# The first layer's mixing steps in another order, and a first softmax unit that needs only its own head's keys

## The chip, the cores and the metric

The kernel runs on one core of a Trainium2 chip. A core has a matrix engine (TensorE, in the profile PE, its weight loads PEld), a vector engine (VectorE, DVE), a scalar engine (ScalarE, ACT), a general engine (GpSimd, POOL) and a queue engine for transfers (SyncE, SP). ACT and POOL can issue transfers as well, from their own instruction queues. The metric is the device time of one execution in microseconds; the median of several runs is compared.

## The reference, cut to what matters

Two layers work on 512 latent tokens and 256 context tokens of width 1024, in float32. Each layer modulates both token sets, mixes them in three ways side by side, and then runs an MLP of width 4096.

```python
def trunk_layer(x, cx, c, c_ctx, rows, cols, w_mod, b_mod, g_mix, w_in, ..., update_ctx):
    sh1, sc1, ga1, sh2, sc2, ga2 = modulation(c, w_mod, b_mod)
    sh1c, sc1c, ga1c, sh2c, sc2c, ga2c = modulation(c_ctx[None], w_mod, b_mod)
    u = (rmsnorm(x, g_mix) * (1 + sc1) + sh1) @ w_in
    uc = (rmsnorm(cx, g_mix) * (1 + sc1c) + sh1c) @ w_in
    p, gq, gk, gv, gg, rf, rb, aq, ak, av = split_in(u)
    ...
    o_gc, s_f, s_b = gla_bidir(*gla_features(gqc, gkc, gvc, rfc, rbc, w_gate, b_gate), s_zero, s_zero)
    o_gl, _, _ = gla_bidir(*gla_features(gq, gk, gv, rf, rb, w_gate, b_gate), s_f, s_b)
    ...
    mix = jnp.concatenate([pool_mixer(p, w_pool, s_pool),
                           gla_output(o_gl, gg, g_gla, x.dtype),
                           latent_attention(ql, k_all, v_all)], axis=-1) @ w_out
    x = x + ga1 * mix
    x = x + ga2 * squared_relu_mlp(rmsnorm(x, g_mlp) * (1 + sc2) + sh2, w_up, w_down)
    ...
```

The modulation is `silu(c) @ w_mod + b_mod`, six vectors of 1024. The gated linear attention (GLA) has four heads of 64 and a data-dependent decay in both directions; the softmax attention has eight query heads and two key heads, with norms and rotary positions. The context is updated in the first layer only.

## The kernel before, in words

Float32 products are made from a high part and a low part of each operand: three matmuls per tile, of hi and hi, hi and lo, lo and hi. Weights come by SP into a `raw` buffer (three of them, 128 x 1024), ACT rounds them into a `hi` buffer, DVE subtracts into a `lo` buffer (five of each); this is `wload`, and its lines are L159 (ACT) and L78 (DVE). Most other tiles of 128 x 768 are work slots of one pool of 29; the activations hT of a mixing stage occupy 16 of them until the last projection has read them.

The mixing stage of a layer is written as four Python generators, and the string `STEPS[l]` says, letter by letter, which of them makes its next step:

- `a`, the projections: the gates of the GLA (one step each for two halves), keys and values of the softmax attention (k_proj, six token tiles, norm and rotation), its queries (q_proj, twice: Q0 and Q1), and the pooled part (p_proj, twice). A token tile is 24 matmuls of 256 columns (L335).
- `g`, the GLA, for two pairs of heads: `decay` (two steps; tree products on POOL, L681), `levels` (eight steps; a batch of small matmuls at L763, then DVE multiplies decays into queries and keys at L720), `states` (two steps), `outputs` (two steps; ACT at L831 and L835, POOL at L833). The order is decay 0, levels 0, states 0, decay 1, outputs 0, levels 1, states 1, outputs 1.
- `m`, layer 0 only, the modulation's second and third rounds (`modulation_round`, the "first" and "second" modulation round of this mixing stage): 16 steps. A step loads two tiles of 128 x 1024 of `w_mod` (rawm, L188) into a hi and a lo buffer and multiplies them (L190). After eight steps `mod_end` (L194 to L209) adds the bias, transposes the result and stores the gate vectors to DRAM (gaD).
- `t`, the softmax attention: `k_stack` transposes the keys (L979) and splits them into kh and kl (L983 to L986), `q_stack` does so for the queries of two heads (L1073 to L1080, qs), and then come twelve units of scores (L1020, L1021), maximum (L1023), exponential (L1024), transposed probabilities (L1038) and values (L1047). A unit's value part is interleaved with the next unit's scores.

In the string of layer 0 the first `t` first runs all that is left of `a` and of `m`; by the string nine of the 16 modulation steps come there, one after another. The queries and keys of head pair 1 of the GLA (`qk_proj(1, 0)` and `qk_proj(1, 1)`) are projected ahead of the strings in both layers.

The string sets the order of the source, not fully that of the engines: the program is built with `schedule_with_timeline_sim=True`, and the builder places an instruction ahead of earlier ones where by its own reckoning those are not ready. Each engine then runs its list strictly as placed.

PSUM has three pools here: psA with two buffers of two banks (projections by features, levels, key transposes, scores), psB with three of one bank, psC with one (modulation, later the attention's values).

Of the kernel before, what the change touches and what calls it, by code (L numbers as in the profile page):

```python
# [10 lines left out]
F32 = mybir.dt.float32  # L11
F32R = mybir.dt.float32r
# [12 lines left out]
LEVELS = (1, 2, 4, 8, 16, 32, 64)  # L25
C_GV, C_GG, C_R, C_AQ = 768, 1024, 1280, 1312
GT = 5
STEPS = ("aggaamgmagagaaagaaaamgaaaaamagaaaagaaaaaagmgaaaagamggmggmgtt"
         "mggtttmtttgttgtmgtggtttgtttgttmgtmtgttmgtt",
         "ggggagaggaaagaaggaaaaaagaaaagaaaggaagaaggatatgatttttgaatgttg"  # L30
         "tttgggtttgttggttttgtttgt")


@with_exitstack
def hybrid_kernel(ctx, tc, x, c, cx, c_ctx, w_mod, b_mod, g_mix, w_in, w_pool, s_pool, w_gate, b_gate,
# [16 lines left out]
    def nm(s):  # L52
        uid[0] += 1
        return f"{s}_{uid[0]}"

    def slot(s, dt=F32, w=NT):
        return sp.tile([128, w], dt, tag="S", name=nm(s))
# [19 lines left out]
    def sub_lo(lo, full, hi):  # L77
        V.tensor_tensor(lo, full, hi.bitcast(F32), ALU.subtract)  # L78
# [113 lines left out]
        mod_end(l, r, modT, pm)  # L192

    def mod_end(l, r, modT, pm):  # L194
        brow = lay.tile([128, 512], F32, tag="brow", name=nm("brow"))
        for j in range(4):
            c0 = r * 2048 + j * 512
            nc.scalar.dma_start(brow[32 * j:32 * j + 32], b_mod[l, c0:c0 + 512].partition_broadcast(32))
        V.tensor_tensor(brow, pm, brow, ALU.add)
        pt = psC("pt")  # L200
        for cc in range(4):
            T.transpose(pt[:, cc * 128:(cc + 1) * 128], brow[:, cc * 128:(cc + 1) * 128], ident)
        V.tensor_copy(modT[:, r], pt.rearrange("p (c j r) -> p j c r", c=4, j=4)[:, :, :, 0:2])
        if r >= 1:
            which = r - 1
            for s in range(2):
                for jj in range(2):
                    row = 32 * (jj + (2 if r == 2 else 0)) + s
                    nc.scalar.dma_start(gaD[l, which, s:s + 1, jj * 512:(jj + 1) * 512], brow[row:row + 1, :])  # L209

    def modulation_sums(l, r, modT, streams):

# [201 lines left out]
    for l in range(2):  # L414
# [195 lines left out]
        for t in alltiles:  # L610
# [3 lines left out]
                ps = psB("tm")  # L614
                tm_matmul(ps[:, 0:288], t, wk, hT, KT)
            A.activation(GU[:, t], ps[:, 0:288], AF.Copy)
        if l == 0:
            qk_proj(1, 0)
            qk_proj(1, 1)

        rT = gp.tile([32, NT], F32, tag="gt", name=nm("rT"), bufs=GT)
        ps = psA("rT")
        for t in alltiles:
            T.transpose(ps[0:32, t * 128:(t + 1) * 128], GU[:, t, 256:288], ident)
        A.activation(rT, ps[0:32, 0:NT], AF.Copy)
        if l == 1:
            qk_proj(1, 0)
            qk_proj(1, 1)

        if l == 0:  # L630
            load_params(1)
# [297 lines left out]
            yield  # L929

        def a_thread():
            for th in (gate_proj(0), gate_proj(1), k_proj(), q_proj(0), q_proj(1), p_proj(0), p_proj(1)):
                yield from th

# [38 lines left out]


        kst = []
        def k_stack():
            ps = psA("kT")
            for t in alltiles:
                T.transpose(ps[:, t * 128:(t + 1) * 128], UKt[0][:, t * 128:(t + 1) * 128], ident)  # L979
            for kv in range(2):  # L980
                kh, kl = slot("kh", F32R), slot("kl", F32R)
                src = ps[64 * kv:64 * kv + 64, 0:NT]
                A.activation(kh[0:64], src, AF.Copy)  # L983
                sub_lo(kl[0:64], src, kh[0:64])
                A.activation(kh[64:128], src, AF.Copy)
                G.tensor_copy(kl[64:128], kl[0:64].bitcast(F32))  # L986
                kst.append((kh, kl))


        nunits = 0  # L990
# [78 lines left out]
        def q_stack(hp):  # L1069
            mix_new(4 + hp)  # L1070
            pq = [psB("qT"), psB("qT")] if both else [psB("qT")]
            for t in live:
                T.transpose(pq[t // 4][:, (t % 4) * 128:(t % 4 + 1) * 128], qview(t, hp), ident)  # L1073
            for hh in range(2):
                qs = slot("qs", F32R)
                for i, pq_ in enumerate(pq):
                    n0, n1 = (0, NL) if i == 0 else (NL, NT)
                    src = pq_[64 * hh:64 * hh + 64, 0:n1 - n0]
                    A.activation(qs[0:64, n0:n1], src, AF.Copy)
                    sub_lo(qs[64:128, n0:n1], src, qs[0:64, n0:n1])  # L1080
                qst[hp * 2 + hh] = qs

        def att_thread():
            k_stack()
            yield
            q_stack(0)
            yield
            nonlocal nunits
            units = [(hp, q0) for hp in range(4) for q0 in ((0, 2, 4) if both else (0, 2))]
            nunits = len(units)  # L1090
            prev = iter(())
            for n, (hp, q0) in enumerate(units):
                P = []
                for i, _ in enumerate(softmax_part(n, hp, q0, P)):
                    for _ in range(2 if i < 2 else 1):
                        next(prev, None)
                    yield
                run(prev)
                if q0 == 0 and hp < 3:
                    q_stack(hp + 1)  # L1100
                prev = value_part(n, hp, q0, P)
                next(pool_, None)
                yield
            yield from prev
            run(pool_)
# [4 lines left out]
        for ch in STEPS[l]:  # L1110
            if ch == "t":
                run(at_)
                run(mods)
            next(ths[ch], None)
        run(at_)
        run(mods)
# [205 lines left out]
```

## Time and profile before

| | |
|---|---|
| median of 3 runs | 1700.56 us (1696.95 to 1703.03) |
| profiled execution | 1700.61 us, of which the span from first to last instruction 1698.8 us |
| HBM read, written | 157.31 MB, 4.23 MB |
| bias loads (L198) in the whole kernel | 20, each 317 to 546 ns on ACT's queue |
| stores of gate vectors (L209) | 16, each 222 to 275 ns on ACT's queue |

In rows of instructions the columns are start and length in us, engine, line, operation, output and inputs with their shapes, and in brackets the idle time before it and what ended it. In rows of waits they are the engine and line, what was waited for, the sum in us, the number of waits and the longest. In rows of groups they are line, engine, operation, tiles, count, then busy us and mean ns, then idle us before them. A matmul's length is from its start to its modelled end, and neighbours overlap, so that the sum of starts counts and not the sum of lengths.

### The profile page before, as it was taken

Reading aid. Unit: us, or ns where it says so; the run is one execution under the profiler, and the core shown is the slowest. Engines: PE = TensorE matmul, PEld = TensorE weight load, DVE = VectorE, ACT = ScalarE, POOL = GpSimd, SP = SyncE. Lnnn points to the kernel's source line nnn. Section 1 sums busy time; section 2 is a strip of 40 time slices with the busy share of each in tenths; the row PEclk is TensorE's granted clock in tenths of the full one; section 3 lists DMA queues with packets and bytes.
Section 4 is the critical chain, followed back from the end, with each engine's and each line's share of the span. In section 5 each row is a group of like instructions: output and inputs, shape, how many; then the busy total and the mean of one; then the engine's idle time right before and its main releaser. Section 6 shows DMA issues by size and latency. Waiting matters only on the chain.

```text
span 1698.8 us, 28409 instructions
## 1 busy us (share of the span) xinstructions
PE 1618.9 (95%) x11899; PEld 1334.4 (79%) x11899; DVE 911.1 (54%) x1302; ACT 639.1 (38%) x1092; POOL 408.3 (24%) x468
## 2 busy tenths in 40 slices
PE   7999968899999999999999999997899999999997
PEld 4989636669978888888888888885669888888885
DVE  4437367753583546546555564486753545545454
ACT  5444246662442312213122234454662522222222
POOL 1111031202201231220311362242111212222225
PEclk9999989999999999999999999997999999999999
DMA  9422530204331313325334232100024223333321
GB/s 320 125 87 65 204 107 3 101 13 127 98 122 53 124 54 121 130 63 186 119 98 161 87 104 81 55 2 1 2 98 126 86 76 99 99 100 99 100 99 50
DMA packets 140255, 163.36 MB, mean 96 GB/s; under 512 B 9412, under 2 KB 116304, under 8 KB 140128
## 3 DMA queue, kind: packets, MB, share of 16 engines
q1 hardware_dynamic: 133312, 147.10, 27.2%
q10 hardware_dynamic: 6816, 14.46, 2.4%
q8 instruction: 93, 1.52, 0.4%
q14 instruction: 34, 0.28, 0.1%
HBM read 157.31 MB, written 4.23 MB: 95 GB/s over the span
## 4 chain that ended last, share of the span: by engine, by line
PE 88%; DVE 4%; ACT 3%; DMA 2%; issue 2%; POOL 1%; SPq 0%; POOLq 0%; DVEq 0%; ACTq 0%
PE dn L335 25%; PE up L316 19%; PE tm L335 8%; PE op L335 7%; PE up L318 5%; PE fm L316 4%; PE av L1047 3%; PE pT L1038 3%; PE up L325 2%; PE fm L318 2%; PE sc L1020 1%; DMA rawm<-in_w_mod_dram 1%; PE att L763 1%; PE pm L190 1%; PE sc L1021 1%
## 5 line engine op out<-in xcount | busy, mean ns | idle before, releaser
L159 ACT ACTIVATE whi<-raw 128x1024 fp32r<-128x1024 f32 (+2 forms) x182 | 184.9, 1031 | 581.2 <-PE dn L335 294.5
L1177 POOL TENSOR_TENSOR X<-X,rtmp 128x512 f32<-128x512 f32 x158 | 215.8, 1368 | 653.5 <-DVE rtmp L1176 653.1
L78 DVE TENSOR_TENSOR wlo<-raw,whi 128x1024 fp32r<-128x1024 f32 (+2 forms) x182 | 224.9, 1245 | 240.2 <-ACT whi L159 237.2
L1176 DVE TENSOR_TENSOR rtmp<-dn,ga 128x512 f32<-128x512 f32 x160 | 109.5, 688 | 215.9 <-PE dn L335 213.0
L335 PE MATMUL dn<-whi,al 128*128 128x512 f32 x480 | 187.2, 390 | 0.0
L335 PE MATMUL dn<-whi,ah 128*128 128x512 f32 x480 | 187.1, 390 | 0.0
L335 PE MATMUL dn<-wlo,ah 128*128 128x512 f32 x480 | 186.3, 390 | 0.0
L316 PE MATMUL up<-h2h,whi 128*128 128x512 f32 x464 | 182.6, 394 | 1.5 <-ACT relu L1219 1.5
L316 PE MATMUL up<-h2h,wlo 128*128 128x512 f32 x464 | 183.2, 395 | 0.0
L316 PE MATMUL up<-h2l,whi 128*128 128x512 f32 x464 | 182.8, 394 | 0.0
L335 PEld LDWEIGHTS dn<-whi,ah 128*128 128x128 f32 x480 | 90.2, 188 | 20.3 <-DVE rtmp L1176 0.8
L316 PEld LDWEIGHTS up<-h2h,whi 128*128 128x128 f32 x464 | 87.1, 188 | 23.5 <-ACT relu L1219 2.5
L335 PEld LDWEIGHTS dn<-whi,al 128*128 128x128 f32 x480 | 90.1, 188 | 19.5
L335 PEld LDWEIGHTS dn<-wlo,ah 128*128 128x128 f32 x480 | 90.1, 188 | 18.9
L316 PEld LDWEIGHTS up<-h2l,whi 128*128 128x128 f32 x464 | 87.1, 188 | 21.8 <-issue 2.5
L335 PE MATMUL tm<-whi,hTh 128*128 128x256 f32 (+1 forms) x352 | 102.3, 291 | 1.1 <-ACT UV L885 1.1
L316 PEld LDWEIGHTS up<-h2h,wlo 128*128 128x128 f32 x464 | 87.2, 188 | 19.6
L335 PE MATMUL tm<-whi,hTl 128*128 128x256 f32 (+1 forms) x352 | 100.8, 287 | 0.0
L335 PE MATMUL dn<-whi,a 128*128 128x512 f32 x320 | 100.0, 395 | 0.4 <-DVE rtmp L1176 0.4
L335 PE MATMUL tm<-wlo,hTh 128*128 128x256 f32 (+1 forms) x352 | 100.0, 287 | 0.0
L335 PE MATMUL op<-whi,mixh 128*128 128x256 f32 x320 | 91.2, 285 | 0.9 <-ACT whi L159 0.9
L335 PE MATMUL op<-wlo,mixh 128*128 128x256 f32 x320 | 90.2, 283 | 0.3 <-DVE wlo L78 0.3
(289 smaller groups left out, 3480.5 us busy)
## 6 DMA issues: line engine op xcount, KB each, us to landing
rawm<-in_w_mod_dram SPq DMA_DIRECT2D x80, 512.0 KB
raw<-in_w_up_dram SPq DMA_DIRECT2D x64, 512.0 KB
raw<-in_w_down_dram SPq DMA_DIRECT2D x64, 512.0 KB
raw<-in_w_in_dram SPq DMA_DIRECT2D x26, 512.0 KB
rawm<-in_w_mod_dram SPq DMA_DIRECT2D x32, 256.0 KB
raw<-in_w_out_dram SPq DMA_DIRECT2D x16, 512.0 KB
raw<-in_w_in_dram SPq DMA_DIRECT2D x12, 256.0 KB
ga<-gaD ACTq DMA_DIRECT2D x6, 512.0 KB
```

Of the source, the lines that this page charges most:

```text
L78: V.tensor_tensor(lo, full, hi.bitcast(F32), ALU.subtract)
L159: A.activation(hi, raw, AF.Copy)
L190: T.matmul(pm[32 * j:32 * j + 32, :], sstat[:, k, :], raw[:, (j % 2) * 512:(j % 2) * 512 + 512], start=(k == 0), stop=(k == KT - 1), skip_ ...
L316: T.matmul(ps[:, 0:NL], a, b[:, 0:NL], start=st, stop=sp_)
L318: T.matmul(ps[:, NL:NT], a, b[:, NL:NT], start=st, stop=sp_)
L325: T.matmul(ps[:, cs], a, b[:, cs], start=(k == 0 and i == 0), stop=(k == nk - 1 and i == 2))
L335: T.matmul(ps, a[:, sl], bb, start=(k == 0 and i == 0), stop=(k == nk - 1 and i == 2))
L763: T.matmul(ps[g * bw:(g + 1) * bw, o0:o0 + bw], a_, b_, start=True, stop=True)
L1038: T.transpose(pt_[:, i * 128:(i + 1) * 128], p_[:, ki * 128:(ki + 1) * 128], ident)
L1047: T.matmul(av_[64 * hh:64 * hh + 64, 0:256], vst, pe[:, hh * 256:hh * 256 + 256], start=(ki == 0), stop=(ki == len(kts) - 1))
L1176: V.tensor_tensor(tmp, ps, ga[0 if t < 4 else 1][:, sl], ALU.mult)
L1177: (V if b == NB - 1 and not both and t == 3 else G).tensor_tensor(X[t][:, sl], X[t][:, sl], tmp, ALU.add)
```

## The change

Four things are changed.

1. `qk_proj(1, 0)` and `qk_proj(1, 1)` become the first two steps of the projections' generator. In layer 1 the string begins with `aa` and is otherwise as before, so that nothing else moves there. In layer 0 the string is new: it deals projections, GLA steps and modulation steps out in turn, all 16 modulation steps and 19 steps of the GLA (with the generator's empty first one 20 letters: decay 0, levels 0, states 0, decay 1, outputs 0 and levels 0 to 2 of pair 1) before the first `t`. The first `t` no longer runs the modulation to its end.
2. `mod_end` takes its 128 x 512 tile for the bias from the `raw` buffers of the weights and loads it by SP's queue instead of ACT's; the stores of gate vectors go by POOL's queue instead of ACT's. This is for all five rounds that use `mod_end`, three of them during layer 0's MLP.
3. `k_stack` is cut in two: the transposes with the stack of the first key head, then `q_stack(0)`, and in the next step the stack of the second key head. In both layers.
4. `q_stack` asks for both heads' tiles at once and stacks the latent part of both heads before their context part.

```diff
-STEPS = ("aggaamgmagagaaagaaaamgaaaaamagaaaagaaaaaagmgaaaagamggmggmgtt"
-         "mggtttmtttgttgtmgtggtttgtttgttmgtmtgttmgtt",
-         "ggggagaggaaagaaggaaaaaagaaaagaaaggaagaaggatatgatttttgaatgttg"
-         "tttgggtttgttggttttgtttgt")
+STEPS = ("agamagamgaamgaagmaagmagamagamagamagamagamagamagamagamgaamgaagmaagmagamagamttgtgttg"
+         "tgttgtttgttgttttgttttgtt",
+         "aaggggagaggaaagaaggaaaaaagaaaagaaaggaagaaggatatgatttttgaatgt"
+         "tgtttgggtttgttggttttgtttgt")
...
     def mod_end(l, r, modT, pm):
-        brow = lay.tile([128, 512], F32, tag="brow", name=nm("brow"))
+        brow = wp.tile([128, 1024], F32, tag="raw", name=nm("brow"), bufs=3)[:, 0:512]
         for j in range(4):
             c0 = r * 2048 + j * 512
-            nc.scalar.dma_start(brow[32 * j:32 * j + 32], b_mod[l, c0:c0 + 512].partition_broadcast(32))
+            nc.sync.dma_start(brow[32 * j:32 * j + 32], b_mod[l, c0:c0 + 512].partition_broadcast(32))
...
-                    nc.scalar.dma_start(gaD[l, which, s:s + 1, jj * 512:(jj + 1) * 512], brow[row:row + 1, :])
+                    nc.gpsimd.dma_start(gaD[l, which, s:s + 1, jj * 512:(jj + 1) * 512], brow[row:row + 1, :])
...
-        if l == 0:
-            qk_proj(1, 0)
-            qk_proj(1, 1)
...
-        if l == 1:
-            qk_proj(1, 0)
-            qk_proj(1, 1)
...
         def a_thread():
+            for qk in range(2):
+                qk_proj(1, qk)
+                yield
             for th in (gate_proj(0), gate_proj(1), k_proj(), q_proj(0), q_proj(1), p_proj(0), p_proj(1)):
                 yield from th
...
-        def k_stack():
+        kT = []
+
+        def k_transposes():
             ps = psA("kT")
             for t in alltiles:
                 T.transpose(ps[:, t * 128:(t + 1) * 128], UKt[0][:, t * 128:(t + 1) * 128], ident)
-            for kv in range(2):
-                kh, kl = slot("kh", F32R), slot("kl", F32R)
-                src = ps[64 * kv:64 * kv + 64, 0:NT]
-                A.activation(kh[0:64], src, AF.Copy)
-                sub_lo(kl[0:64], src, kh[0:64])
-                A.activation(kh[64:128], src, AF.Copy)
-                G.tensor_copy(kl[64:128], kl[0:64].bitcast(F32))
-                kst.append((kh, kl))
+            kT.append(ps)
+
+        def k_stack(kv):
+            kh, kl = slot("kh", F32R), slot("kl", F32R)
+            src = kT[0][64 * kv:64 * kv + 64, 0:NT]
+            A.activation(kh[0:64], src, AF.Copy)
+            sub_lo(kl[0:64], src, kh[0:64])
+            A.activation(kh[64:128], src, AF.Copy)
+            G.tensor_copy(kl[64:128], kl[0:64].bitcast(F32))
+            kst.append((kh, kl))
...
             for hh in range(2):
-                qs = slot("qs", F32R)
-                for i, pq_ in enumerate(pq):
-                    n0, n1 = (0, NL) if i == 0 else (NL, NT)
+                qst[hp * 2 + hh] = slot("qs", F32R)
+            for i, pq_ in enumerate(pq):
+                n0, n1 = (0, NL) if i == 0 else (NL, NT)
+                for hh in range(2):
+                    qs = qst[hp * 2 + hh]
                     src = pq_[64 * hh:64 * hh + 64, 0:n1 - n0]
                     A.activation(qs[0:64, n0:n1], src, AF.Copy)
                     sub_lo(qs[64:128, n0:n1], src, qs[0:64, n0:n1])
-                qst[hp * 2 + hh] = qs
 
         def att_thread():
-            k_stack()
+            k_transposes()
+            k_stack(0)
+            q_stack(0)
             yield
-            q_stack(0)
+            k_stack(1)
             yield
...
             if ch == "t":
                 run(at_)
-                run(mods)
             next(ths[ch], None)
```

More of the change, by code (lines that the diff above doesn't have):

```diff
@@ L27 @@
 GT = 5
-STEPS = ("aggaamgmagagaaagaaaamgaaaaamagaaaagaaaaaagmgaaaagamggmggmgtt"
-         "mggtttmtttgttgtmgtggtttgtttgttmgtmtgttmgtt",
-         "ggggagaggaaagaaggaaaaaagaaaagaaaggaagaaggatatgatttttgaatgttg"
-         "tttgggtttgttggttttgtttgt")
+STEPS = ("agamagamgaamgaagmaagmagamagamagamagagamagamagamagamgaamgaagmaagmagamagamttgtgttg"
+         "tgttgtttgttgttttgttttgtt",
+         "aaggggagaggaaagaaggaaaaaagaaaagaaaggaagaaggatatgatttttgaatgt"
+         "tgtttgggtttgttggttttgtttgt")
 @with_exitstack
```

## The prediction

> **What bounds the kernel now.** I began with the page: its span, its first section and its chain of work that ended last.
>
> ```profile
> span 1698.8 us, 28409 instructions
> PE 1618.9 (95%) x11899; PEld 1334.4 (79%) x11899; DVE 911.1 (54%) x1302; ACT 639.1 (38%) x1092; POOL 408.3 (24%) x468
> ...
> PE 88%; DVE 4%; ACT 3%; DMA 2%; issue 2%; POOL 1%; SPq 0%; POOLq 0%; DVEq 0%; ACTq 0%
> ```
>
> TensorE is the bound. The change removes no matmul, so it can only win time in which PE stands still or runs slowly. The view of windows shows where that is (length; busy us of PE, PEld, DVE, ACT, POOL; granted clock; DMA share; GB/s).
>
> ```profile
> 490.00:1000.00 510.00, 510.00 (x2558) 424.98 (x2557) 269.18 (x283) 119.54 (x134) 123.32 (x95) 1.00 0.33 110
> ...
> 90.00:235.70 145.70, 141.69 (x1862) 110.14 (x1860) 68.95 (x135) 56.53 (x106) 25.06 (x50) 0.98 0.39 131
> 235.70:246.90 11.20, 0.00 (x0) 0.03 (x1) 10.99 (x15) 8.23 (x12) 6.34 (x7) 0.60 0.03 10
> 246.90:383.40 136.50, 124.15 (x1406) 86.70 (x1406) 89.07 (x156) 85.63 (x204) 22.90 (x41) 0.95 0.11 38
> ...
> 1035.00:1145.00 110.00, 107.88 (x1211) 95.50 (x1210) 59.16 (x112) 54.42 (x106) 30.32 (x52) 1.00 0.15 44
> ...
> 1182.00:1276.00 94.00, 87.72 (x928) 59.87 (x924) 62.06 (x114) 60.16 (x133) 12.45 (x18) 0.99 0.14 51
> ```
>
> The MLP of layer 0 (490 to 1000) has no gap. Layer 0's mixing has three pieces. In A, the projections (90 to 235.7), PE idles 145.70 - 141.69 = 4.0 us and a clock of 0.98 costs about 2.9 us. In B (235.7 to 246.9) PE does nothing. In C, the attention (to 383.4), it idles 136.50 - 124.15 = 12.35 us; a clock of 0.95 loses 6.8 us, of which I put 5.5 on matmuls (an estimate: the rest falls into idle time). The last two rows are the same two stages in layer 1. PE's waits up to 480 us say for what:
>
> ```profile
> PE sc L1020 <- DVE qs L78: 11.2, 1, 11.2
> PE sc L1020 <- ACT p L1024: 5.1, 4, 1.9
> ...
> PE pm L190 <- DMA rawm<-in_w_mod_dram: 3.9, 3, 3.5
> ```
>
> The largest is the first score matmul's wait for the stacked queries. The timeline shows how they came late: PE's rows first, then ACT's, then DVE's.
>
> ```profile
> 225.08 0.77 PE L979 MATMUL kT<-ident,UK 128*128 128x128 f32 x5
> ...
> 234.63 1.06 PE L763 MATMUL att<-QQ,KK 64*32 64x32 f32 x96
> 246.90 0.77 PE L1020 MATMUL sc<-kh,qs 128*128 128x512 f32 x1 [11.21 <-DVE qs L78]
> ```
>
> ```profile
> 231.20 1.16 ACTq L209 DMA_DIRECT2D gaD<-brow  x4
> 232.96 0.87 ACT L831 ACTIVATE ogl<-rg 128x512 f32<-128x512 f32 x2 [3.91 <-DMA gaD<-brow]
> ...
> 237.04 0.84 ACT L835 ACTIVATE mixh<-ogl 128x768 fp32r<-128x768 f32 x1 [2.82 <-POOL ogl L833]
> ...
> 238.76 0.78 ACT L983 ACTIVATE kh<-kT 64x768 fp32r<-64x768 f32 x1
> ...
> 244.38 0.86 ACT L1079 ACTIVATE qs<-qT 64x512 fp32r<-64x512 f32 x2
> ```
>
> ```profile
> 246.07 1.02 DVE L78 TENSOR_TENSOR qs<-qT,qs 64x512 fp32r<-64x512 f32 x2
> ```
>
> The keys lay transposed in PSUM at 225.85, but ACT split them off only at 238.76. Ahead of that in ACT's order stood the gate-output of head pair 0, held 3.91 us by the modulation's store (gaD), then 2.82 us by POOL. After it came both heads' keys, then the queries at 244.38, while DVE (10.99 of 11.20 us busy) grew the decay levels of pair 1. All that falls between the last projection and the first scores because layer 0's order leaves decay 1, output 0, the whole second modulation round and all levels of pair 1 until the projections are over.
>
> **The change, part by part.** The sum is made against the profiled execution: 1700.61 us, its span 1698.8 and 1.8 around it. The median of the runs shown is 1700.56, so no correction is needed.
>
> Stage A. The new order spreads the 16 modulation steps, decay 1, output 0 and levels 0 to 2 of pair 1 among the projections. PE's work without loss is 141.69 - 2.9 = 138.8 us. Of the levels only the third is new here, since the first two ran before 235.7 already; one level is 8.3/8 = 1.04 us by this group of eight:
>
> ```profile
> L763 PE MATMUL att<-QQ,kc 64*32 64x32 f32 x768 | 8.3, 200 | 2.2 <-ACT p L1024 1.3 <-DVE dg L783 0.9
> ```
>
> Layer 1 already interleaves the same gate levels and projections, and PE loses 2.1 us in its 110; scaled to A that is 2.8 us. A becomes 138.8 + 1.0 + 2.8 = 142.6, so **3.1 us** are won (bounds: no stall at all, 5.9; today's 6.9 us of loss again, -1.0).
>
> Weights. They share the hi and lo buffers, five each, with the modulation tiles. Today most modulation tiles come after the weights; now four or five pairs of them are asked for between two sets of weights, so the second half of Q0's and of Q1's weights gets its buffer only when a modulation step is done. Then ACT and DVE still have to convert:
>
> ```profile
> L78 DVE TENSOR_TENSOR wlo<-raw,whi 128x1024 fp32r<-128x1024 f32 x7 | 8.7, 1243 | 17.3 <-ACT whi L159 17.3
> ...
> L159 ACT ACTIVATE whi<-raw 128x1024 fp32r<-128x1024 f32 x7 | 7.4, 1058 | 15.1 <-PE fm L318 10.2 <-PE tm L335 3.4 <-PE pm L190 1.2
> ```
>
> That is 1.06 + 1.24 = 2.3 us, beside which PE has a level or a modulation step of about 1 us. I charge 1 us at each of two places, **-2 us** (bounds 0, and 2.3 at each of four sets, -9.2).
>
> Stage B. Output 0 and the store are now finished well before the keys, and the first unit needs only head pair 0's keys. No row of layer 0 shows this; the nearest is the same spot of layer 1, where output 0 is nearly out of the way but both keys still come first (PE, ACT, DVE, POOL):
>
> ```profile
> 1158.80 0.92 PE L979 MATMUL kT<-ident,UK 128*128 128x128 f32 x6 [2.89 <-ACT pm L927]
> ...
> 1165.05 0.76 PE L1020 MATMUL sc<-kh,qs 128*128 128x512 f32 x1 [4.51 <-DVE qs L78]
> ```
>
> ```profile
> 1159.76 0.80 ACT L983 ACTIVATE kh<-kT 64x768 fp32r<-64x768 f32 x1 [0.53 <-PE kT L979]
> ...
> 1162.39 0.81 ACT L983 ACTIVATE kh<-kT 64x768 fp32r<-64x768 f32 x1
> 1163.22 0.59 ACT L1079 ACTIVATE qs<-qT 64x512 fp32r<-64x512 f32 x1
> ```
>
> ```profile
> 1160.59 0.95 DVE L78 TENSOR_TENSOR kl<-kT,kh 64x768 fp32r<-64x768 f32 x1 [4.33 <-ACT kh L983]
> 1163.22 0.96 DVE L78 TENSOR_TENSOR kl<-kT,kh 64x768 fp32r<-64x768 f32 x1 [1.69 <-ACT kh L983]
> 1164.22 0.69 DVE L78 TENSOR_TENSOR qs<-qT,qs 64x512 fp32r<-64x512 f32 x1
> ```
>
> ```profile
> 1161.67 0.82 POOL L986 CAST kl<-kl 64x768 fp32r<-64x768 f32 x1 [2.06 <-DVE kl L78]
> ```
>
> Without the second key (ACT at 1162.39, DVE at 1163.22) the scores can start when POOL's copy ends, 1161.67 + 0.82 = 1162.5, instead of 1165.05. So 2.5 of the 4.51 us go there and 2.0 stay; the second key then stands in the way of the second score instead, since it holds one of two PSUM buffers. For layer 1 I take **2.0 us** (bounds: 2.5, and -1.0 where the second key's DVE step delays a unit instead). For layer 0 the same wait of 2.0, and 0.3 for its fuller queues, replaces 11.2: **8.9 us** (bounds: all 11.2 go, or the 4.51 of layer 1 and as much again remain, 2.2).
>
> Stage C. Work without loss is 124.15 - 5.5 = 118.6, less the level moved to A, 117.6. Layer 1's attention idles 94.00 - 87.72 = 6.3 us per 87.7 busy; that ratio gives 8.4. The first unit has no values of an earlier one beside it; today it waits four times for ACT's exponentials, 5.1 us in sum, and I keep 3.4. For a slow clock after B's gap I keep 2.5. C becomes 117.6 + 8.4 + 3.4 + 2.5 = 131.9 against 136.5, **4.6 us** (bounds: 10.5, with neither of the last two, and -3.1, as three levels fewer are there to fill PE's waits).
>
> A gap of 3.47 us for a modulation tile at 181.19 is followed by a granted clock below one:
>
> ```profile
> 173.00:190.00 17.00, 13.09 (x189) 7.38 (x189) 8.80 (x19) 4.65 (x15) 2.66 (x6) 0.80 0.76 275
> ```
>
> [...]
>
> At nothing I cost three things. The bias loads move from ACT's queue to SP's and into a raw weight buffer; behind them on SP stand the next modulation and weight loads. In the MLP they find PE 510.00 us busy of 510.00 with weights converted ahead; without that cover each of five rounds would wait about a conversion, 2.3 us, 11.5 in all. The stores move to POOL (four took ACT's queue 1.16 us, the row at 231.20), where decay products and rope products stand behind them; the first scores need neither. Pair 1's early decay takes four of the 29 work slots while hT holds 16, so output 0 waits for a slot until level 0 of pair 1 has read its queries; its result is due only at the output projection (384 us).
>
> [...]
>
> Sum: 3.1 - 2 + 8.9 + 4.6 + 2.0 = 16.6 us; 1700.6 - 16.6 = **1684.0 us**.
>
> **The rivals.** *Slower: the modulation runs in lockstep with its buffers.* Two weights in use and two converted early leave one of five buffers, so each step's load starts only when the step before has left PE. The slowest such load and three projection tiles of PE are, in the chain:
>
> ```profile
> 140.80 8.82 PE tm L335 x72
> ...
> 173.14 8.00 DMA rawm<-in_w_mod_dram
> ```
>
> Between two steps PE has two tiles and a level, 2 x 2.94 + 1.04 = 6.9 us, against 8.00: 1.1 us of waiting at 16 steps, 17.6, and the conversions at -9.2 instead of -2. The gains without weights are 18.6; 26.8 against them is 8.2 us slower, **1709**. It decides from 18.6 us of PE waits for modulation tiles and weights. Against it: three buffers stay free of two weights in use, and DMA moved 275 GB/s in the window above while only one wait of 3.47 us came.
>
> *No change: the stall moves.* The order in the source isn't PE's order: the key transposes ran at 225.08 among modulation steps that stand before them in the source. If the builder again puts ACT's and DVE's level work ahead of the stacks, B keeps about 10 us and C its waits; A's 3.1 - 2, layer 1's 2.0 and 1 of B leave 4.1, **1696.5**. For it: DVE was 10.99 of 11.20 busy there. Against: three of the eight levels are then done.
>
> *Better: all of it.* A 5.9, B 11.2, C 10.5, layer 1 2.5: 30.1 us, **1670**. Against it: the first unit's waits for ACT are its own.
>
> **How the numbers follow.** A measurement of this kernel tells about 0.3% from no change, 5.1 us, that is 1695.5 to 1705.7. The forecast (1676 to 1695) gets 0.54, better than that 0.12, no change 0.20, slower 0.14. Faster is 0.54 + 0.12 = 0.66. The range leaves out about 0.07 below and 0.13 above: 1672 to 1702, which holds the no-change case and the bounds of A, B and the weights; the forecast's own is 1676 to 1695.
>
> **What would show it.** Right: no row "sc <- DVE qs" over 4 us in either layer, the key split (L983's successor) soon after the key transposes, modulation steps of 1 us among the projections without DMA waits over 3 us, C's clock at 0.97 or more. Wrong: PE waits for rawm or for wlo before the attention that add to over 10 us (weights and lockstep); a gap over 8 us before the first scores (B); a gap in the MLP of layer 0 (raw buffer); scores that begin 10 us earlier and an attention that ends at the same time (C).

## The result, and the profile after

The changed kernel takes 1689.49 us (median of seven executions) against 1700.56 us of the kernel before on the same chip. Six of the seven lie between 1686.68 and 1691.56 us; one took 8777.98 us and is left out of the ratio, as is one of e11's twelve below (2748.11 us). The ratio is 0.9937, with a 95% interval of 0.9919 to 0.9954: some 10.7 us faster, where 16.6 were forecast. The profiled execution took 1691.56 us. The lines of its page that answer to those of before:

```profile
span 1689.7 us, 28426 instructions
...
PE 1621.0 (96%) x11899; PEld 1334.7 (79%) x11899; DVE 908.4 (54%) x1302; ACT 639.0 (38%) x1092; POOL 416.0 (25%) x484
...
PE 88%; DVE 4%; ACT 3%; DMA 2%; issue 2%; POOL 1%; SPq 0%; POOLq 0%; DVEq 0%; ACTq 0%
```

PE has the same 11899 matmuls and is busy 2 us longer, in a span that is 9.1 us shorter. So what went is idle time. The windows of the same stages (length; busy us of PE, PEld, DVE, ACT, POOL; granted clock; DMA share; GB/s):

```profile
90.00:232.65 142.65, 140.59 (x2056) 110.47 (x2054) 80.84 (x152) 63.72 (x116) 35.05 (x59) 1.00 0.39 131
232.65:236.20 3.55, 0.42 (x4) 0.24 (x3) 3.36 (x10) 2.52 (x5) 0.82 (x1) 0.88 0.01 1
236.20:258.30 22.10, 15.09 (x370) 11.61 (x370) 16.46 (x30) 12.01 (x30) 2.72 (x8) 0.65 0.01 3
258.30:372.50 114.20, 107.50 (x846) 73.09 (x844) 67.16 (x116) 73.28 (x172) 21.49 (x37) 1.00 0.13 47
236.20:372.50 136.30, 122.60 (x1212) 84.70 (x1212) 83.62 (x145) 85.29 (x201) 24.20 (x45) 0.94 0.11 40
474.00:990.00 516.00, 516.00 (x2591) 430.32 (x2590) 272.73 (x286) 120.00 (x135) 126.72 (x103) 1.00 0.34 111
```

The projections (first row) took 142.65 us instead of 145.70, the stretch almost without matmuls ahead of the scores 3.55 instead of 11.20. The attention is cut in two here: from the first score to the first value product (the first softmax unit), and from there to the output projection; the row after these two has both together. The first part is the poor one: PE busy 15.09 of 22.10 us, at a clock of 0.65. The MLP has no gap, as before. In the kernel before the first unit was shorter, and it held fewer instructions:

```profile
246.90:261.60 14.70, 10.44 (x136) 8.43 (x136) 13.89 (x24) 7.54 (x17) 0.72 (x4) 0.73 0.01 3
```

So the scores begin 10.7 us earlier (246.90 against 236.20), but the first value product only 3.3 us earlier (261.6 against 258.3). By the output projection the lead is 11.8 us again (its first matmul stands at 384.28 before and at 372.53 after), since the five levels that ran beside the later units in the kernel before are now behind.

The stretch ahead of the scores, in the timeline of PE and then of ACT:

```profile
229.09 0.87 PE L978 MATMUL kT<-ident,UK 128*128 128x128 f32 x6
229.80 1.25 PE L1074 MATMUL qT<-ident,Uq 128*128 128x128 f32 x10
...
234.93 0.41 PE L1074 MATMUL qT<-ident,Uq 128*128 128x128 f32 x2 [2.28 <-DVE qs L78]
236.19 0.77 PE L1021 MATMUL sc<-kh,qs 128*128 128x512 f32 x1 [0.85 <-DVE dg L777]
```

```profile
230.00 0.80 ACT L984 ACTIVATE kh<-kT 64x768 fp32r<-64x768 f32 x1 [1.88 <-PE kT L978]
230.70 0.85 ACT L1082 ACTIVATE qs<-qT 64x512 fp32r<-64x512 f32 x2
```

ACT now takes the keys 0.04 us after their transposes (230.00; the matmuls end at 229.96), where it came 12.9 us late before. What remains is 2.28 us for the last two query transposes, whose PSUM buffer DVE must empty first, and 0.85 us for a level's buffer. A head pair has six query transposes, so ten and two are those of pairs 0 and 1, and the last two belong to pair 1, which the first unit doesn't need. They aren't what the first score waited for in the end: psA has two buffers, one holds the keys until the second key head is split, the other a level, and DVE empties the level's at 235.41 + 0.64 = 236.05, just ahead of the score at 236.19.

```profile
235.41 0.64 DVE L777 COPY_PREDICATED dg<-mask,att 128x192 f32<-128x192 int32 x2
```

And the end of the first unit, ACT and then PE:

```profile
249.15 2.96 ACT L781 ACTIVATE AT<-dg 32x192 f32<-32x192 f32 x8 [1.14 <-DVE dg L777]
252.14 0.90 ACT L1025 ACTIVATE p<-sc,nmx 128x768 f32<-128x768 f32 x1
252.94 0.19 ACT L1025 ACTIVATION_READ_ACCUMULATOR p<-sc,nmx 128x1 f32 x1
253.03 2.16 ACT L770 ACTIVATE AT<-att 32x192 f32<-32x192 f32 x8
```

```profile
253.18 0.90 PE L1039 MATMUL pT<-ident,p 128*128 128x128 f32 x3 [2.65 <-ACT p L1025]
```

Eight copies of a decay level (AT, 2.96 us) stand in ACT's order ahead of the unit's last exponential, and PE waits 2.65 us for it. Then eight more copies follow. By the trace the last four levels of pair 1 run in this unit; in the kernel before only one level did. Of the 7.40 us by which the unit grew (14.70 to 22.10), 4.65 are busy time of PE, most of it the three more levels' own matmuls (all levels' in the unit: 5.43 us here, 1.02 before), and 2.75 are waits.

### The profile page after: what moved, and what is told of

The parts are those of the page before. It is cut to its first block, busy times and chain, and to the rows that moved or that the text cites. A ratio compares the mean times of both kernels' runs of the same rounds, so it can differ in the third digit from the quotient of the medians.

```text
span 1689.7 us, 28426 instructions
## 1 busy us (share of the span) xinstructions
PE 1621.0 (96%) x11899; PEld 1334.7 (79%) x11899; DVE 908.4 (54%) x1302; ACT 639.0 (38%) x1092; POOL 416.0 (25%) x484
## 4 chain that ended last, share of the span: by engine, by line
PE 88%; DVE 4%; ACT 3%; DMA 2%; issue 2%; POOL 1%; SPq 0%; POOLq 0%; DVEq 0%; ACTq 0%
PE dn L335 25%; PE up L316 19%; PE tm L335 8%; PE op L335 7%; PE up L318 5%; PE fm L316 4%; PE av L1048 3%; PE pT L1039 3%; PE up L325 2%; PE fm L318 2%; PE sc L1021 1%; PE att L757 1%; PE sc L1022 1%; PE pm L190 1%; DMA rawm<-in_w_mod_dram 1%
```

## The experiments

All ratios are to the kernel before, run beside them. The columns of marks are PE's start times in layer 0 of each kernel's profiled execution, in us: first key transpose, first score, first value product, first matmul of the output projection.

| kernel | us | ratio, 95% interval | kT | score | value | output |
|---|---|---|---|---|---|---|
| before | 1700.56 | 1 | 223.8 | 246.9 | 261.6 | 384.3 |
| changed | 1689.49 | 0.9937 [0.9919, 0.9954] | 229.1 | 236.2 | 258.3 | 372.5 |
| e1 order alone | 1686.03 | 0.9937 [0.9922, 0.9952] | 224.8 | 231.8 | 254.2 | 368.6 |
| e2 split alone | 1697.42 | 0.9994 [0.9983, 1.0004] | 219.2 | 237.9 | 256.8 | 381.5 |
| e3 bias tile and queues alone | 1696.34 | 0.9988 [0.9977, 0.9999] | 218.9 | 240.3 | 254.6 | 378.2 |
| e4 changed, no split | 1686.80 | 0.9941 [0.9927, 0.9954] | 227.6 | 235.3 | 257.6 | 372.8 |
| e5 levels later | 1682.35 | 0.9897 [0.9884, 0.9911] | 228.4 | 231.9 | 247.9 | 368.5 |
| e6 levels first | 1692.98 | 0.9961 [0.9947, 0.9975] | 243.9 | 251.5 | 261.6 | 377.4 |
| e7 modulation late | 1684.58 | 0.9913 [0.9900, 0.9925] | 219.9 | 229.1 | 252.5 | 369.4 |
| e8 old GLA order | 1692.83 | 0.9963 [0.9950, 0.9977] | 220.7 | 236.9 | 255.1 | 378.4 |
| e9 levels later, modulation late | 1675.66 | 0.9873 [0.9857, 0.9889] | 220.0 | 223.6 | 243.0 | 359.9 |
| e10 as e5, no split | 1686.84 | 0.9939 [0.9924, 0.9954] | 232.0 | 238.1 | 252.6 | 374.0 |
| e11 second key late | 1697.10 | 0.9999 [0.9989, 1.001] | 228.8 | 232.4 | 258.0 | 379.8 |
| e12 as e9, no split | 1674.89 | 0.9863 [0.9847, 0.9880] | 219.9 | 227.1 | 242.1 | 358.9 |

The medians of the rows are from different rounds, so that only the ratios are compared. A mark is from one execution.

### Which part of the change gives the gain: e1 to e4

**e1** is the kernel before with the two strings and the projections moved into their generator; **e2** has the split of the key and query stacks alone; **e3** has the bias tile and the queues alone; **e4** is the changed kernel with the stacks as before.

```diff
--- e1: before, with STEPS of the changed kernel, and
...
         def a_thread():
+            for qk in range(2):
+                qk_proj(1, qk)
+                yield
...
--- e2: before, plus
...
-            k_stack()
+            k_transposes()
+            k_stack(0)
+            q_stack(0)
             yield
-            q_stack(0)
+            k_stack(1)
...
--- e3: before, plus
-        brow = lay.tile([128, 512], F32, tag="brow", name=nm("brow"))
+        brow = wp.tile([128, 1024], F32, tag="raw", name=nm("brow"), bufs=3)[:, 0:512]
...
-            nc.scalar.dma_start(brow[32 * j:32 * j + 32], b_mod[l, c0:c0 + 512].partition_broadcast(32))
+            nc.sync.dma_start(brow[32 * j:32 * j + 32], b_mod[l, c0:c0 + 512].partition_broadcast(32))
...
-                    nc.scalar.dma_start(gaD[l, which, s:s + 1, jj * 512:(jj + 1) * 512], brow[row:row + 1, :])
+                    nc.gpsimd.dma_start(gaD[l, which, s:s + 1, jj * 512:(jj + 1) * 512], brow[row:row + 1, :])
```

> The new strings and the two projections in the generator alone; the bias tile, its queues and the key and query stacks as before. My theory (most of the gain is the gap before the first scores of layer 0, made by what the old order left for that place): 8 to 10 us faster than before, ratio 0.994 to 0.995, no wait of the first score over 5 us in layer 0, and layer 1 as before. Rival, the queues (ACT was held by the store of the gate vectors): without moving the stores the gain is under 4 us. Rival, the split: under 4 us as well, the gap in layer 0 still over 8 us.

> The split of the key stack and the new order inside the query stack alone, in the old strings. My theory: 2 us from layer 1 and at most 2.5 from layer 0, so 2 to 4 us faster, ratio 0.9975 to 0.999; the gap before the first scores of layer 0 stays over 8 us. Rival, the split carries the change: over 7 us faster, ratio under 0.996, gap in layer 0 under 6 us.

> The bias tile in a raw weight buffer by SP and the stores by POOL alone, in the old strings and stacks. My theory: within 2 us of before (ratio 0.999 to 1.001), since ACT's wait of 3.9 us for the store is only one link of the chain. Rival, the queues carry the change: over 5 us faster, ratio under 0.997. Rival, the raw buffer costs: slower by 2 us or more, with waits of PE in layer 0's MLP or mixing that before did not have.

> The changed kernel with the key and query stacks as before the change. My theory: 2 to 4 us slower than the changed kernel, that is a ratio to before of 0.995 to 0.9965, first score of layer 1 again 5 us after the key transposes. Rival, the gain of the split is given back within the first unit: the same as the changed kernel within 1 us, ratio 0.993 to 0.9945, though the first score comes later.

The order alone has the whole gain: e1 has the ratio of the changed kernel, a little better than was expected of it. PE's largest wait for scores in it (columns: sum, times, longest):

```profile
PE sc L1017 <- DVE qs L78: 3.5, 1, 3.5
```

The 11.2 us of before are 3.5 with both keys still ahead of the queries. The split alone (e2) makes nothing that can be measured, where 2 to 4 us were expected, though its first score comes earlier than before; its gap waits for keys instead:

```profile
PE sc L1024 <- ACT kh L989: 7.5, 2, 7.0
PE sc L1024 <- ACT p L1028: 7.1, 5, 2.6
```

In e2 143.6 us pass from the first score to the output projection (381.5 - 237.9), against 137.4 before, with PE idle for 19.0 of them instead of 13.2: what the earlier start gives is spent in waits, most of them for ACT. Taking the split out of the changed kernel (e4) changes nothing that can be told from the noise either. The queues and the bias tile (e3) cost nothing; the 2 us that they seem to bring are at the edge of the interval. In e3 the gap is still there, and ACT stands as long ahead of the gate-output as before, though the stores have left its queue:

```profile
226.71 0.87 ACT L831 ACTIVATE ogl<-rg 128x512 f32<-128x512 f32 x2 [3.79 <-PE rg L827]
...
240.32 0.76 PE L1020 MATMUL sc<-kh,qs 128*128 128x512 f32 x1 [10.55 <-DVE qs L78]
```

So the 3.91 us that ACT waited there before were not the store's doing, though the profile's row named it: without the store there, ACT waits 3.79 us for PE. The three ratios of e1, e2 and e3 don't add up exactly to the whole, and need not: the builder places every list anew.

### What fills the first unit: e5 and e6

Both are the changed kernel with layer 0's string altered from the first `t` on, or just before it. In e5 the last five levels come only after eight steps of the attention, in e6 they come before the first `t`.

```diff
-STEPS = ("agamagamgaamgaagmaagmagamagamagamagagamagamagamagamgaamgaagmaagmagamagamttgtgttg"
-         "tgttgtttgttgttttgttttgtt",
--- e5
+STEPS = ("agamagamgaamgaagmaagmagamagamagamagagamagamagamagamgaamgaagmaagmagamagamtttttttt"
+         "gttgttgttgttgttgttgttgttgtt",
--- e6
+STEPS = ("agamagamgaamgaagmaagmagamagamagamagagamagamagamagamgaamgaagmaagmagamagamgggggt"
+         "ttttttttttgttgttttgttttgtt",
```

> The changed kernel, but levels 3 to 7 of pair 1 come after the first unit of the softmax and then one GLA step per two steps of it. My theory now (five levels among the first unit's scores hold its exponentials on ACT, so that the first value matmul comes 22 us after the first score instead of 14.7 as before): first value at most 15 us after the first score, attention from first score to output projection under 134 us, 2 to 5 us faster than the changed kernel, ratio to before 0.990 to 0.992. Rival, this stage takes some 137 us whatever stands in it first: within 1.5 us of the changed kernel, ratio 0.993 to 0.9945.

> The changed kernel, but all eight levels of pair 1 before the first softmax step (five more, one after another behind the last projection). The attention from first score to output projection falls under 131 us by my theory; the five levels are 5.2 us on PE, and 14 us where each waits for DVE's products. So between 1 us faster and 5 us slower than the changed kernel, ratio 0.993 to 0.9965, with the first score 6 to 14 us later. Rival, the stage takes 137 us whatever stands in it: 6 us slower or more, ratio over 0.997.

e5 is faster than the changed kernel, by 0.004 (0.9897 against 0.9937, the intervals apart). Its first unit takes 16.00 us instead of 22.10, with one level left in it by the trace, as in the kernel before:

```profile
231.90:247.90 16.00, 11.30 (x134) 8.73 (x134) 14.05 (x26) 9.17 (x19) 3.54 (x10) 0.68 0.01 2
```

The unit is nearly as short as expected (at most 15 us); the whole attention isn't shorter (136.6 us from first score to output projection, where under 134 was expected), because the levels are done later. What is won up to the output projection are the 4 us by which the scores begin earlier: the level whose buffer the first score waited for isn't there. The ratio says some 7 us; the rest lies behind layer 0's attention, whose source is the same, and isn't explained.

e6 shows the other price. Without levels the attention shrinks to 125.9 us, but the scores begin at 251.5, 15 us later than in the changed kernel, since PE, which has no other work left, waits for the levels' own chain:

```profile
PE sc L1021 <- ACT AT L770: 4.6, 1, 4.6
...
PE att L757 <- DVE QQ L714: 3.3, 4, 1.2
```

Of the three places tried, the levels are best beside units that have value products to run, not before the scores and not inside the first unit.

### Where the modulation steps stand: e7, e8 and e9

e7 keeps the first eight letters `m` of the changed string and puts the other ten together just before the first `t`. e8 keeps the modulation spread out, but goes back to the old order of projections and GLA. e9 has both the late modulation of e7 and the late levels of e5.

```diff
-STEPS = ("agamagamgaamgaagmaagmagamagamagamagagamagamagamagamgaamgaagmaagmagamagamttgtgttg"
-         "tgttgtttgttgttttgttttgtt",
--- e7
+STEPS = ("agamagamgaamgaagmaagmagamagamagamagagaagaagaagagaagaagaagagaagammmmmmmmmmttgtg"
+         "ttgtgttgtttgttgttttgttttgtt",
--- e8
+STEPS = ("aaamggamagamgagmaaamgaamaagmaaamaaamgaamaagmaaamaaamggamaaamgagmgggmgamttggtttttt"
+         "gttgtgtggtttgtttgttgttgttgtt",
--- e9
+STEPS = ("agamagamgaamgaagmaagmagamagamagamagagaagaagaagagaagaagaagagaagammmmmmmmmmtttttttt"
+         "gttgttgttgttgttgttgttgttgtt",
```

> The changed kernel with projections and GLA steps in the same order, but only the first eight modulation letters in their places and the rest right before the first softmax step. My theory: spreading the modulation is worth the wait at 174 to 190 us of before, so 3 to 6 us slower than the changed kernel, ratio 0.9955 to 0.9975, with waits of PE for modulation tiles of over 5 us. Rival, the GLA's order gives all of it: within 1.5 us of the changed kernel, ratio 0.993 to 0.9945.

> The changed kernel with the old order of projections and GLA steps (the two projections first), and all modulation steps spread evenly before the first softmax step. My theory: the gap before the first scores is back (over 6 us), 5 to 8 us slower than the changed kernel, ratio 0.9965 to 0.9985. Rival, spreading the modulation gives all of it: within 1.5 us of the changed kernel.

> The changed kernel with both orders that were faster alone: levels 3 to 7 of pair 1 after the first softmax unit, and ten of the modulation steps together just before the scores. Theory A: the two act at different places (the first unit, and the projections), so their 7 and 5 us add: ratio .986 to .989. Theory B: both put TensorE work that needs no ACT beside the first unit, once by keeping the levels away and once by modulation steps: ratio .989 to .991, no better than the levels alone.

e7 was expected slower or the same, and came out faster than the changed kernel (0.9913 against 0.9937; the intervals share 0.9919 to 0.9925). So where the GLA has its new order, dealing the modulation out among the projections adds nothing. e8 has the old order of projections and GLA, in which decay 1 and output 0 still come after the last projection. It was expected to be 5 to 8 us slower than the changed kernel, and keeps 6.3 us of gain (0.0037 of 1697), with a gap before the scores of 5.4 us:

```profile
PE sc L1021 <- DVE qs L78: 5.4, 1, 5.4
```

The new order of the GLA is thus worth some 4.4 of the 10.7 us by this pair, and it takes the time from first key transpose to first score down from 16.2 to 7.1 us, as the forecast said of its stage B. More than half of the gain stands without it. In e8 all modulation steps are out of the way before the first `t`, and e7 has its whole gain with most of them still late: the two orders stand in for each other in part, and what each is worth alone was not measured (e8 has the split and the queues as well, which alone bring at most 2 us, by e2 and e3).

e9 shows what the modulation steps are good for. Its windows, from the first key transpose to the first score and the first unit:

```profile
220.00:223.60 3.60, 2.42 (x23) 2.18 (x21) 3.11 (x7) 2.42 (x5) 2.02 (x4) 1.00 0.95 359
223.60:243.00 19.40, 19.13 (x212) 9.54 (x212) 15.61 (x30) 10.10 (x20) 5.66 (x14) 1.00 0.46 168
```

PE's timeline at the start of that unit:

```profile
223.57 0.49 PE L1021 MATMUL sc<-kh,qs 128*128 128x512 f32 x1 [1.18 <-ACT kh L986]
224.00 4.50 PE L190 MATMUL pm<-rawm,sstat 128*32 128x512 f32 x40
...
229.04 1.05 PE L190 MATMUL pm<-rawm,sstat 128*32 128x512 f32 x4
```

PE is busy 19.13 of 19.40 us at full clock, against 15.09 of 22.10 at 0.65 in the changed kernel. The modulation's matmuls read tiles as they come from HBM (rawm) and need nothing of ACT or DVE until their bias at the end (in this unit PE waited for them once, 0.24 us for a tile); the builder put eight such steps (64 of these matmuls up to 237.25) into the pauses in which the first unit waits for maximum and exponential. They left the projections, so the scores begin 8.3 us earlier than in e5, and the output projection 8.6 us earlier. The gains of e5 and e7 (7 and 4 us beyond the changed kernel by their ratios) come together in 0.9873: the forecast that they add was right. Its reason, that the two act at different places, was right in part only, since the modulation steps do their good inside the first unit too.

### The split again: e10, e11 and e12

e10 is e5, and e12 is e9, each with the stacks as before the change (e4's edit). e11 is the changed kernel with the second key transposed again and stacked only when head pair 1 begins, so that it holds nothing during the first unit.

```diff
--- e11: changed, plus
             q_stack(0)
             yield
-            k_stack(1)
-            yield
...
+                if hp == 1 and q0 == 0:
+                    k_transposes()
+                    k_stack(1)
                 if q0 == 0 and hp < 3:
                     q_stack(hp + 1)
```

> The levels after the first unit, and the stacks of keys and queries as before the change (both keys before the first score). Theory A: the split was given back because the five levels were what the first unit waited for; with the levels gone its 2 to 4 us show: ratio .991 to .9925 here, slower than with the split. Theory B: the second key's split costs the same wherever it stands, before the first score or between the first and second: within .001 of the kernel with the split (.989 to .9905), with a first score 2 to 4 us later and an attention shorter by as much.

> The changed kernel, but the second key head is transposed again and stacked only when head pair 1 begins, long after the first unit, so that it holds no PSUM buffer, ACT or DVE there. Theory A (the second key's split in the first unit is what gives the split back): first unit 2 to 3 us shorter, ratio .991 to .9925. Theory B (the levels and their copies on ACT set the first unit's length): no difference from the changed kernel, .993 to .9945, or up to .996 for the six more transposes and a wait where pair 1 begins.

> The fastest kernel so far (levels after the first unit, ten modulation steps together just before the scores: .9873), with the stacks of keys and queries as before the change. The split was worth nothing in two pairs of kernels and .004 in one. Theory A (it is worth 1.5 to 2 us in each layer from key transposes to output projection, once the first unit waits for nothing else): ratio .989 to .991, stage 1.5 us or more longer in each layer. Theory B (modulation steps now stand beside the first unit and cover the second key): ratio .987 to .988, no difference.

e11 is as slow as the kernel before, which neither theory had. It answers the question it was made for all the same: its scores begin 3.8 us earlier than in the changed kernel (232.4), and its first value comes at 258.0, just as there (258.3) and in e4 (257.6).

```profile
232.40:258.00 25.60, 15.92 (x370) 12.65 (x370) 19.13 (x38) 13.09 (x33) 2.99 (x8) 0.65 0.01 2
258.00:379.80 121.80, 111.49 (x853) 74.57 (x851) 68.30 (x118) 75.04 (x174) 21.84 (x38) 0.97 0.13 47
```

Whether the second key is split before the first score, after it, or much later, the first unit ends at 258 with four levels inside. From the first key transpose to the first value it takes 29.2 to 30.0 us in the four kernels with this string (e1, changed, e4, e11), wherever the second key is split, and 19.6 and 20.6 in e5 and e10, which have one level there. So the levels set that end, not the keys; how much of it is their work on DVE, their copies on ACT or their matmuls on PE was not separated. Why the rest of its attention takes 121.80 us instead of 114.20 (3.6 more idle, 4.0 more busy at a clock of 0.97 instead of 1.00), of which six transposes are under 1 us, was not found.

e10 is 0.0042 slower than e5, more than expected of the split, and e12 is not slower than e9 (0.9863 and 0.9873, intervals overlapping). In e10 3.6 us are lost already ahead of the first key transpose (232.0 against 228.4), where no instruction of the stacks has run; from there to the output projection it is 142.0 against 140.1 us. So some 2 us in layer 0 agree with the split, and the rest with another placement of the projections, which was not pursued. In e12 the modulation covers the keys: its score comes 3.5 us later than in e9, and PE works through the wait.

```profile
219.90:227.10 7.20, 6.75 (x62) 3.32 (x60) 4.92 (x12) 5.08 (x8) 4.51 (x9) 1.00 0.80 273
227.10:242.10 15.00, 14.97 (x174) 8.26 (x170) 12.68 (x22) 6.97 (x16) 3.12 (x8) 1.00 0.43 172
```

In three of four pairs the split makes no difference that can be told from the noise. e9 and e12 are the fastest kernels of this study, some 22 us below the kernel before.

## Why the prediction was right, and which term was wrong

The sign, the place and the range were right, the size was 5.5 us too good. Of the signs named, one failed: C's clock was to be at 0.97 or more, and is 0.94. The terms, measured on the profiled executions:

| term | predicted | measured |
|---|---|---|
| A, projections | 3.1 won with one more level inside | 145.70 to 142.65, 3.05 won, with two more |
| weights | 2 lost | one wait of 0.9 us (below) |
| B, gap before the scores | 8.9 won | 11.20 to 3.55, 7.65 won |
| C, attention | 4.6 won | 137.4 to 136.3 from first score to output projection, 1.1 won |
| layer 1 | 2.0 won | 2.25 won up to the first score, then lost again |
| the rest | nothing | some 2.6 lost between layer 0's output projection and layer 1's keys, and at the end |

The last row is what is missing to the 9.1 us between the two spans; one execution each can't tell it from the noise. That the sum still fell inside the range owes something to luck: the 2 us charged for weights, which weren't lost, make up for more than half of what C lacks.

**A** was right, and the loss of 2 us for weights and lockstep wasn't there. All waits of PE up to 480 us that bear on it in the changed kernel:

```profile
PE pm L190 <- DMA rawm<-in_w_mod_dram: 1.4, 1, 1.4
...
PE fm L316 <- ACT whi L159: 0.9, 1, 0.9
```

Of the 18.6 us of such waits from which the rival *lockstep* would decide, 2.3 came. One part of the reasoning was not needed, though: e7 and e9 have long rows of modulation steps together and are faster.

**B** was right in its mechanism, shown by e1 (order alone, gap 3.5) and in part by e8: with the old GLA order the gate-output stands ahead of the keys on ACT again, and 16.2 us pass from the first key transpose to the first score. But PE's gap there is only 5.4, so the rest of the 11.2 went with the other parts of the change. The rival *the stall moves* (about 10 us kept) is out. The store, to which the forecast gave 3.91 us of ACT's delay, had no part in it (e3). What remains was sized 2.3, as layer 1's wait for queries, and is 3.55; it ends with a level's PSUM buffer, and PE in e5, without that level, has no wait over 1.2 us before its first score. The split of the first head's keys, to which the forecast gave part of the gain, isn't needed for it, as e1 shows.

**C is the step that failed.** It was put as 117.6 of work, 8.4 of idle time, 3.4 for the first unit's waits and 2.5 for a slow clock. After the first unit it held: 114.20 - 107.50 = 6.7 idle, 1.7 better than thought. In the first unit PE idled 22.10 - 15.09 = 7.0 us instead of 3.4. And PE's busy time is 15.09 + 107.50 = 122.6, where one more level moved out should have left 116.6: 6.0 us instead of the 2.5 for a slow clock. I had taken the first unit over as it was, with its four waits for exponentials. By the new order it came together with four levels that need ACT and DVE as it does, and so it grew by 7.4 us (14.70 to 22.10). e5 leaves one level there and has 16.00; e11 shows that the second key doesn't set the end. The bound of C, which said that "three levels fewer are there to fill PE's waits", doesn't hold for the first unit: with three levels more in it, PE's idle time there rose from 4.26 to 7.01 us.

**Layer 1.** The first score came after the key transposes by 1152.88 - 1148.88 = 4.00 us, where it had been 6.25; that is the 2.0 us of the forecast:

```profile
1148.88 0.87 PE L978 MATMUL kT<-ident,UK 128*128 128x128 f32 x6 [2.89 <-ACT pm L921]
...
1152.88 0.80 PE L1021 MATMUL sc<-kh,qs 128*128 128x512 f32 x1 [2.36 <-ACT dg L773]
```

From the first score to the output projection it then took 116.5 us instead of 114.1. In the other kernels that have the split this stretch is 112.6 to 114.8 (e2, e5 to e9), in those without it 111.9 to 116.0 (before, e1, e3, e4, e10, e12), so how much is given back can't be said from one execution each. From the key transposes to the output projection layer 1 takes 118.4 us on average in the seven kernels with the split and 120.3 in the six without it (e11 left out), with single ones from 116.6 to 122.2. That agrees with the 2.0; the times of e2 and e4 show no gain, but their intervals don't exclude it. The term stays open.

**The costs put at nothing** held: the MLP's 516 us have no gap, and the stores and bias loads (e3) cost no time.

```profile
L209 POOL DMA_DIRECT2D gaD<-brow x16: 484/486/725, 162.8 to 949.5; - x16
...
DMA to landing us min/median/max: 1.6/2.6/4.0
```

(Columns of the first row: least, median and largest ns, first and last start.) A store took 0.48 to 0.73 us of POOL instead of 0.22 to 0.28 of ACT, and landed after 4.0 us at most. Whether single stores waited in that time, these rows don't tell.

One thing did stand behind the stores on POOL, where the forecast had nothing that the first scores need: the copy of the first head's keys, ready at 231.78 by DVE's row of 230.83 (POOL's rows first).

```profile
230.65 1.98 POOL L209 DMA_DIRECT2D gaD<-brow  x4 [12.46 <-DVE brow L199]
232.68 0.82 POOL L987 CAST kl<-kl 64x768 fp32r<-64x768 f32 x1
...
230.83 0.95 DVE L78 TENSOR_TENSOR kl<-kT,kh 64x768 fp32r<-64x768 f32 x1 [0.48 <-ACT kh L984]
```

It was 0.9 us late, and cost nothing here, because the level's buffer held the score until 236.05.

## What to carry to other kernels

A latency-bound stretch (here the first softmax unit, where each step waits for VectorE's maximum and ScalarE's exponential) wants filler that uses only the engine that waits: matmuls on operands that are there, as the modulation's were in e9 (PE busy 19.13 of the unit's 19.40 us). With filler that runs through the same engines, four decay levels instead of one, the unit took 22.10 us here instead of 14.70, and PE idled 7.01 us of it instead of 4.26. Holding that back shortened the unit to 16.00 us (e5), though not the attention as a whole (136.6 us against 136.3).

Starting a stage earlier is only worth what its end keeps: set the marks at both ends of it, and at the stage's own first result, before a lead is counted as a gain. And of a change in several parts, each is worth its run alone: here one of them held the whole gain that could be measured.

## What the runs showed of the hardware

In the changed kernel the granted clock was 0.50 just behind a stretch of 3.55 us in which PE's longest idle time was 2.28 us. Windows of 3 us, before and at the start of the first unit:

```profile
231.00:234.00 3.00, 1.65 (x101) 1.33 (x100) 2.90 (x7) 2.71 (x6) 2.45 (x5) 1.00 0.06 8
234.00:237.00 3.00, 1.18 (x3) 0.49 (x3) 2.88 (x6) 1.18 (x3) 0.00 (x0) 0.72 0.00 0
237.00:240.00 3.00, 2.07 (x79) 1.69 (x82) 2.58 (x7) 1.67 (x3) 1.52 (x4) 0.50 0.03 5
```

PE was busy 2.83 of the 6 us up to 237, and in the midst of them, from 232.65 to 236.20, 0.42 of 3.55 us, between idle times of 2.28 and 0.85. In the window from 237 on the clock is 0.50. Whether that stretch brought it down, and how little work would be too little, can't be read from the trace. e9 has no such stretch (PE busy 2.42 of the 3.60 us before its scores), and its first unit ran at 1.00.
